# An encoder layer in hi/lo split fp32: the 16x16 substitution of the next head pair becomes a stream of its own, and the state chain of a pair is planned behind it

## The chip, the cores and the metric

The kernel runs on one core of a Trainium2 chip. The metric is device time in microseconds (us), the median of repeated executions. One further execution was profiled, and all rows below come from it.

## The reference, cut to what matters

One layer of a streaming encoder on 576 tokens: 64 that continue a running stream and 512 that open a new one, in nine chunks of 64 tokens. The layer has width 1024, sixteen heads of 64, and everything is in fp32.

```python
h   = rms_norm(x, g_pre_mix)
p   = h @ w_in                    # r, k, v, three low-rank inputs, u, gv, two gates
oA  = rwkv7(p)                    # per head: S = S*w + (S a) b' + v k' ; y = S r
oB  = gmlp(u, gv)                 # spatial gating over 128-frame chunks
m   = sigmoid(gateA) * (oA @ w_proj_a) + sigmoid(gateB) * (oB @ w_proj_b)
x   = x + rms_norm(m @ w_o);  x = x + rms_norm(swiglu(rms_norm(x)))
```

The recurrence of `rwkv7` is computed by chunks. Inside a chunk it needs the inverse of a unit triangular 64x64 matrix per head; between chunks the 64x64 state is carried from one chunk to the next.

## The kernel before, in words

**Products.** Every large product takes three passes on TensorE (PE): each operand is split into a high and a low part, and high x high, low x high and high x low are summed. For the weights, ScalarE (ACT) rounds a raw block to its high part (`whi<-raw`, L302) and GpSimd (POOL) subtracts it in two halves (`wlo<-raw,whi`, L305). One block of 128 columns is 48 matmuls of 288 columns, named `pj` in the first half of the kernel.

**Head pairs.** Heads are worked two at a time, in eight pairs numbered 0 to 7, in roughly the first 520 us; the products `pb`, `gv`, `pa`, `po`, `fg`, `fp` of the rest of the layer follow. For a pair, in order:

- `elementwise`: the decay products `z`, their tanh on ACT (`sg`, `ta`, L666), a running sum along each chunk on VectorE (DVE), `L` (L670), its two exponentials on ACT (`EL` L674, `sg<-L` L676), then `k`, `aq`, `BK`, `AR` and the inner products `am`. DVE masks these into `AB`, and eight DMAs of SyncE (SP) write the diagonal 16x16 blocks of `AB` to DRAM (`d_inv<-AB`, L750).
- `inverse`: SP loads the blocks back, as 80 matrices on 80 partitions (`M`, L855). DVE inverts them by substitution: 15 steps of two small operations, a product `Xt` (L863) and a sum `X` (L866), each dependent on the one before. SP stores `X` to DRAM (L868) and loads it as `IV` in eight DMAs (L872). DVE transposes it (`IT`, L875), and the products `m` (two), `mp`, `mu` build the 64x64 inverse from 16x16 blocks.
- `turns`: transposes on PE (`tb`, `tr`, `tv`) with their copies on ACT (`At`, `Kt`, `Vt`) and DVE (`AB<-tb`, L816), and the products `wv`.
- `batch`: the products `d`, `e`, `c`, `y` of all nine chunks.
- `chain`: the state goes from chunk to chunk. A product `pc` needs the state that DVE's sum before it left (`S`, and `So` for the states that are results, L1005). At the end `py` adds the states' part to the result `Y`.
- `finish`: normalisation and output gate, stored to DRAM.

**What sets the order.** PE's instructions stand in the order in which the class `Weave` writes them. Each of the functions above is a generator, a stream that yields either an estimated time in us, looked up in the table `LAT`, or an event with such a time behind it. `Weave.run` keeps an estimated clock: as long as some stream may go on, it goes on, and otherwise the next matmul of the running weight block is issued as a filler. Nothing of the table exists on the chip; real waits are semaphores. DVE, ACT, POOL and SP get their orders from the framework's scheduler, apart from a few instructions that are pinned, and each runs its queue strictly in that order here.

In the kernel before, `inverse` of pair p+1 holds the substitution too and starts as soon as its `A` event is there (`inv_all`). While the chain of pair p runs, the 30 substitution operations of pair p+1 stand on DVE between the `TD`/`AR` sums of pair p (L966, L967) and the first state sum of the chain (L1005).

Of the kernel before, what the change touches and what calls it, by code (L numbers as in the profile page):

```python
# [20 lines left out]
NPAIR = NH // 2  # L21
# [16 lines left out]
LAT = {  # L38
# [4 lines left out]

# [1 line left out]
}  # L45
# [188 lines left out]
def layer(tc, I, O):  # L234
# [35 lines left out]
    clk = Weave()  # L270
# [110 lines left out]
    d_inv = [tc.dram_tile([2, 2, 64 // SB, 10, SB, SB], F32, name=f"d_inv{g}") for g in range(NPAIR)]  # L381


    EV = [{"hp": p_} for p_ in range(NPAIR)]
# [463 lines left out]
        clk.signal("values", hp_)  # L848


    def inverse(E):

        hp_, AB, di = E["hp"], E["AB"], d_inv[E["hp"]]
        M = rp.tile([P, SB, SB], F32, tag="M", name="M")[0:NU]
        sp.dma_start(M.rearrange("u s t -> u (s t)"), di[0].rearrange("h b u s t -> (h b u) (s t)"))  # L855
        X = rp.tile([P, SB, SB], F32, tag="X", name="X")[0:NU]
        sp.dma_start(X.rearrange("p i t -> p (i t)"), I["cst"][0:NU, C_X0:NCST])
        yield lat("M", hp_)
        tmp = rp.tile([P, SB * SB // 4], F32, tag="Xt", name="Xt")[0:NU]
        for s in range(0, SB - 1):  # L860
            w, r = SB - 1 - s, s + 1
            t3 = tmp[:, 0:r * w].rearrange("u (j t) -> u j t", t=w)
            ins = dve.tensor_tensor(t3, X[:, 0:r, s:s + 1].broadcast_to([NU, r, w]), M[:, s:s + 1, s + 1:SB].broadcast_to([NU, r, w]), ALU.mult)  # L863
            if s == 0:
                tc.keep_in_program_order(ins)
            dve.tensor_tensor(X[:, 0:r, s + 1:SB], X[:, 0:r, s + 1:SB], t3, ALU.add)  # L866
            yield LAT["X"]
        sp.dma_start(di[1].rearrange("h b u s t -> (h b u) (s t)"), X.rearrange("p i t -> p (i t)"))  # L868
        for h in range(2):
            for b in range(64 // SB):  # L870
                r0_ = 64 * h + SB * b
                sp.dma_start(IV[r0_:r0_ + SB, :, SB * b:SB * b + SB], di[1, h, b].rearrange("u s t -> s u t"))  # L872
        blocks = [(64 * h, 64 * h + 32) for h in range(2)]
        quarters = [(64 * h + 32 * b, 32 * b) for h in range(2) for b in range(2)]
        turn = lambda: dve.transpose(IT.rearrange("p c t -> p (c t)"), IV.rearrange("p c t -> p (c t)"))  # L875
        U = AB.rearrange("p j h t -> p (j h) t")
        yield lat("U", hp_)
        if hp_ > 0:
            yield (("d", hp_ - 1), 0.0)

        PT = rp.tile([P, 10, SB], F32, tag="PT16", name="PT16")
        tc.keep_in_program_order(turn())
        yield lat("m1", hp_)
        yield from clk.free()
        pp = ps1("m1", 1.8)[:, 0:10 * SB].rearrange("p (c t) -> p c t", t=SB)
        for u in range(10):
            for r, q in quarters:
                mmul(pp[r:r + 32, u], U[r:r + SB, u, q:q + 32], IT[r:r + SB, u, q:q + SB], start=True, stop=True)
        act.activation(PT, pp, ACT.Copy, scale=low)
        yield lat("m2", hp_)  # L890
        yield from clk.free()
        pp = ps1("m2", 2.2)[:, 0:10 * SB].rearrange("p (c t) -> p c t", t=SB)
        for u in range(10):
            for r, q in quarters:
                mmul(pp[r:r + SB, u], PT[r:r + 32, u, :], IV[r:r + 32, u, q + SB:q + 32], start=True, stop=True)
        for r, q in quarters:
            act.activation(IV[r:r + SB, :, q + SB:q + 32], pp[r:r + SB], ACT.Copy)

        PT = rp.tile([P, 10, 32], F32, tag="PT", name="PT")
        turn()  # L900
        yield lat("mp", hp_)
        yield from clk.free()
        pp = ps1("mp", 1.9)[:, 0:320].rearrange("p (c t) -> p c t", t=32)
        for u in range(10):
            for a0, a1 in blocks:
                mmul(pp[a1:a1 + 32, u], U[a0:a1, u, 32:64], IT[a0:a1, u, 0:32], start=True, stop=True)
        for _, a1 in blocks:
            act.activation(PT[a1:a1 + 32], pp[a1:a1 + 32], ACT.Copy)
        yield lat("mu", hp_)
        yield from clk.free()  # L910
        pp = ps1("mu", 1.9)[:, 0:320].rearrange("p (c t) -> p c t", t=32)
        for u in range(10):
            for _, a1 in blocks:
                mmul(pp[a1:a1 + 32, u], IV[a1:a1 + 32, u, 32:64], PT[a1:a1 + 32, u, :], start=True, stop=True)
        for _, a1 in blocks:
            act.activation(IT[a1:a1 + 32, :, 0:32], pp[a1:a1 + 32], ACT.Copy)
        clk.signal("it", hp_)
# [74 lines left out]
    def chain(E):  # L992


        AR, C, S0, hp_ = (E[n] for n in ("AR", "C", "S0", "hp"))
        add = lambda c: C[:, PLACE[c][1], PLACE[c][0], :]
        state = lambda c: S0 if c == 0 else add(1) if c == 2 else S[:, c, :]
        for n, cs in enumerate([(2, 0)] + [(c,) for c in range(3, NCH)]):
            pc = ps1c("pc").rearrange("p (i v) -> p i v", v=HD)
            for i, c in enumerate(cs):  # L1000
                mmul(pc[:, i], TD[:, c, :], state(c), start=True, stop=True)
            for i, c in enumerate(cs):
                last = c in (0, NCH - 1)
                dst = rp.tile([P, HD], F32, tag="So", bufs=2, name="So") if last else S[:, c + 1, :]
                dve.tensor_tensor(dst, pc[:, i], add(c), ALU.add)  # L1005
                if last:
                    sp.dma_start((O["wkv_s"] if c == 0 else O["wkv_p"])[hp_], dst)
            yield LAT["S"]

        yield (("wide", hp_), LAT["y"])  # L1010
        Y = E["Y"]
        yield from clk.free(2)
        py = [ps1("py", 2.2)[:, 0:320].rearrange("p (j v) -> p j v", v=HD) for _ in range(2)]
        for c, j, half_ in PLACES2:
            for h, rows in enumerate(HR):
                mmul(py[h][HR[half_], j], AR[rows, 1, c * 64:(c + 1) * 64], state(c)[rows], start=True, stop=True, skip_group_check=True)
        for h in range(2):
            dve.tensor_tensor(Y[:, :, HR[h]], py[h], Y[:, :, HR[h]], ALU.add)
        clk.signal("chain", hp_)
# [45 lines left out]
    def elem_all():  # L1065
# [13 lines left out]
        for i in range(2):  # L1079
            sp.dma_start(R["ln"][i][0:64], I["rows"][i:i + 1, :].broadcast_to([64, D]))  # L1080

    def inv_all():
        for p_ in range(NPAIR):
            yield (("A", p_), 0.0)
            yield from inverse(EV[p_])

    def turn_all():
        for p_ in range(NPAIR):
            yield (("A", p_), 0.0)
            yield from turns(EV[p_])  # L1090

    def batch_all():
        for p_ in range(NPAIR):
            yield from batch(EV[p_])

    def chain_all():
        for p_ in range(NPAIR):
            yield (("inv", p_), LAT["ch0"])
            yield from chain(EV[p_])

    def fin_all():
        for p_ in range(NPAIR):
            yield (("chain", p_), 0.0)
            yield from finish(EV[p_])
# [235 lines left out]
    def norm2(h):  # L1340
        hs = HS[h]
        yield (("y", h), 0.0)
        for j in range(8):
            square_sum(mix_q, R["acc2"], y[j][:, hs], j == 0, hs, (dve, pool)[h])
            yield LAT["sq"]
        yield LAT["rs"]
        b = yield from rstd_row(R["fp"], R["acc2"], STARTS[h], "r2")
        act.activation(R["rs2"][:, hs], b, ACT.Copy)
        clk.signal("rs2", h)
# [170 lines left out]
    with tc.manual_schedule(engines={mybir.EngineType.PE}):  # L1520
        lora = {0: lora_w(lora_raw(0), pin=False)}
        for nm, b in (("k", BLK_K), ("r", BLK_R), ("v", BLK_V)):
            take = Shifted(b, nm, scale=True)
            EV[0][nm] = [take(h, raw0[nm][:, HS[h]]) for h in range(2)][1]
            clk.signal(nm, 0)
        clk.run(chain_all(), fin_all(), batch_all(), inv_all(), turn_all(), elem_all(), norm1(0), norm1(1), norm2(0), norm2(1), hidden(), oa_all(), ob_all(),
                ln_all(), norm3(0), norm3(1))
    R["o"].close()
    R["d0"].close()
# [19 lines left out]
```

## Time and profile before

| | us |
|---|---|
| median of 3 runs | 1224.84 |
| lowest and highest run | 1223.98, 1225.69 |
| profiled execution, its own time | 1224.46 |
| its span, first to last instruction | 1222.7 |
| PE busy | 1179.5 |
| POOL busy | 606.8 |
| DVE busy | 524.5 |
| ACT busy | 467.9 |

The own time is what the same execution would report as a run; the span leaves out 1.76 us around the instructions. A busy time is the sum over an engine's instructions, and PE's idle time is mostly made of short waits, which a view of the trace lists by the instruction that ended them.

### The profile page before, as it was taken

What the parts mean: (1) busy time and instruction counts of PE and PEld (TensorE: products, weight loads), DVE (VectorE), ACT (ScalarE), POOL (GpSimd) and SP (SyncE); (2) the same over time, 40 slices, a digit from 0 to 9 for tenths busy, and PEclk for the clock granted to TensorE, in tenths of its full rate; (3) what the DMA queues carried; (4) which work ended last, traced back from release to release, by engine and by line L of the source; (5) the groups of instructions that cost most, each with busy time, mean ns of one, the idle gap of its engine ahead of it and who ended that gap; (6) DMA issues with size and microseconds to landing.
All of it is one profiled execution on the core that took longest, in us unless ns stands there. A gap on an engine that the chain in (4) does not pass through costs nothing.

```text
span 1222.7 us, 29954 instructions
## 1 busy us (share of the span) xinstructions
PE 1179.5 (96%) x12938; PEld 1146.6 (94%) x12938; DVE 524.5 (43%) x1086; ACT 467.9 (38%) x889; POOL 606.8 (50%) x477
## 2 busy tenths in 40 slices
PE   7999999999999999999899999999999999999997
PEld 6999889899998999999899999999999999999996
DVE  5756365656555655432515431753333333300003
ACT  5555534453545453342521333543222222222220
POOL 6675343546363535233545553466555655634442
PEclk9999999999999999999999999999999999999999
DMA  5234223232322223242643541232222222242222
GB/s 186 75 111 106 78 55 94 48 94 50 97 68 76 75 77 87 89 132 77 210 125 122 182 147 55 94 111 81 87 87 79 78 87 86 81 157 83 80 77 78
DMA packets 68276, 118.05 MB, mean 97 GB/s; under 512 B 30832, under 2 KB 36208, under 8 KB 68144
## 3 DMA queue, kind: packets, MB, share of 16 engines
q1 hardware_dynamic: 68000, 116.06, 31.7%
q8 instruction: 101, 1.65, 0.6%
q14 instruction: 31, 0.25, 0.1%
q10 hardware_dynamic: 144, 0.08, 0.0%
HBM read 99.83 MB, written 16.28 MB: 95 GB/s over the span
## 4 chain that ended last, share of the span: by engine, by line
PE 78%; DVE 12%; ACT 4%; issue 3%; POOL 2%; DMA 1%; SPq 0%; DVEq 0%; POOLq 0%; ACTq 0%
PE fg L286 21%; PE pj L286 15%; PE po L286 15%; PE pb L286 4%; PE gv L286 4%; PE pa L286 3%; PE fp L286 2%; DVE X L866 2%; DVE Xt L863 2%; PE am L286 1%; PE z L286 1%; PE m L286 1%; PE pc L286 1%; PE wv L286 1%; PE d L286 1%
## 5 line engine op out<-in xcount | busy, mean ns | idle before, releaser
L305 POOL TENSOR_TENSOR wlo<-raw,whi 128x512 fp32r<-128x512 f32 (+1 forms) x286 | 395.4, 1407 | 344.2 <-ACT whi L302 322.3
L302 ACT ACTIVATE whi<-raw 128x1024 fp32r<-128x1024 f32 x143 | 149.0, 1045 | 282.0 <-PE fg L286 174.9
L1293 DVE TENSOR_TENSOR rs<-rs,nsq 128x288 f32<-128x288 f32 (+2 forms) x12 | 9.0, 752 | 105.9 <-ACT nsq L1292 105.9
L1365 DVE TENSOR_TENSOR ft<-ft,fg 128x288 f32<-128x288 f32 x40 | 16.4, 450 | 68.0 <-PE fg L286 66.5
L1359 DVE TENSOR_TENSOR fg<-fg,rs 128x288 f32<-128x288 f32 x40 | 16.5, 453 | 63.0 <-PE fg L286 62.9
L1362 DVE SCALAR_TENSOR_TENSOR ft<-ft,fg 128x576 f32<-128x576 f32 (+1 forms) x24 | 28.1, 1172 | 18.3 <-ACT ft L1361 18.3
L1363 POOL TENSOR_TENSOR ft<-ft,rs 128x576 f32<-128x576 f32 (+1 forms) x24 | 31.8, 1327 | 6.5 <-DVE ft L1362 5.8
L368 POOL TENSOR_TENSOR rr<-rm,mhalf 128x3 f32<-128x3 f32 (+1 forms) x6 | 5.0, 831 | 51.9 <-DVE rm L367 51.9
L286 PE MATMUL pc<-S,TD 128*128 128x64 f32 x112 | 20.2, 262 | 8.6 <-DVE So L1005 8.6
L688 POOL TENSOR_TENSOR aq<-aq,k 128x576 f32<-128x576 f32 x8 | 11.4, 1425 | 34.4 <-PE pc L286 30.0
L286 PE MATMUL pj<-h1h,whi 128*128 128x288 f32 x88 | 27.8, 316 | 0.0
L286 PE MATMUL pj<-h5h,whi 128*128 128x288 f32 x88 | 27.8, 316 | 0.0
L286 PE MATMUL pj<-h0h,whi 128*128 128x288 f32 x88 | 27.7, 315 | 0.0
L863 DVE TENSOR_TENSOR Xt<-X,M 80x15 f32<-80x15 f32 (+7 forms) x120 | 25.5, 213 | 5.1 <-DMA M<-d_inv 1.5
L286 PE MATMUL pj<-h2h,whi 128*128 128x288 f32 x88 | 27.7, 315 | 0.0
L286 PE MATMUL pj<-h6h,whi 128*128 128x288 f32 x88 | 27.5, 312 | 0.0
L286 PE MATMUL pj<-h7h,whi 128*128 128x288 f32 x88 | 27.3, 311 | 0.0
L286 PE MATMUL pj<-h4h,whi 128*128 128x288 f32 x88 | 27.2, 309 | 0.0
L286 PEld LDWEIGHTS pc<-S,TD 128*128 128x128 f32 x112 | 17.4, 189 | 10.3 <-DVE So L1005 10.3
L866 DVE TENSOR_TENSOR X<-X,Xt 80x15 f32<-80x15 f32 (+7 forms) x120 | 25.3, 210 | 4.1
L1036 POOL TENSOR_TENSOR gm<-gm,mhalf 128x10 f32<-128x10 f32 x8 | 16.1, 2012 | 21.9 <-DVE gm L1035 12.7
L286 PE MATMUL pj<-h3h,whi 128*128 128x288 f32 x88 | 26.8, 305 | 0.0
(1200 smaller groups left out, 4269.6 us busy)
## 6 DMA issues: line engine op xcount, KB each, us to landing
raw<-in_w_in SPq DMA_DIRECT2D x50, 512.0 KB, 3.7
raw<-in_w_gate SPq DMA_DIRECT2D x22, 512.0 KB, 3.6
raw<-in_w_up SPq DMA_DIRECT2D x22, 512.0 KB, 3.6
raw<-in_w_down SPq DMA_DIRECT2D x16, 512.0 KB, 3.5
raw<-in_w_gv SPq DMA_DIRECT2D x8, 512.0 KB, 4.2
raw<-in_w_proj_a SPq DMA_DIRECT2D x8, 512.0 KB, 4.1
raw<-in_w_proj_b SPq DMA_DIRECT2D x8, 512.0 KB, 3.7
raw<-in_w_o SPq DMA_DIRECT2D x8, 512.0 KB, 3.7
```

Source lines behind the costliest of these rows:

```text
L286: return pe.matmul(out, lhsT, rhs, **kw)
L302: keep(act.activation(hi[:, :cols], raw[:, :cols], ACT.Copy))
L305: keep(pool.tensor_tensor(lo[:, c0:c1], raw[:, c0:c1], f(hi[:, c0:c1]), ALU.subtract))
L688: pool.tensor_tensor(aq, aq, k, ALU.mult)
L863: ins = dve.tensor_tensor(t3, X[:, 0:r, s:s + 1].broadcast_to([NU, r, w]), M[:, s:s + 1, s + 1:SB].broadcast_to([NU, r, w]), ALU.mult)
L866: dve.tensor_tensor(X[:, 0:r, s + 1:SB], X[:, 0:r, s + 1:SB], t3, ALU.add)
L1036: pool.tensor_tensor(m, m, mhalf, ALU.pow)
L1293: eng.tensor_tensor(acc[:, hs], acc[:, hs], q[:, hs], ALU.add)
L1359: keep(dve.tensor_tensor(g[:, HS[h]], pg, rs2[:, HS[h]], ALU.mult))
L1362: keep(dve.scalar_tensor_tensor(t[:, ts], t[:, ts], 1.0, g[:, ts], ALU.add, ALU.mult))
L1363: pool.tensor_tensor(t[:, ts], t[:, ts], rs2[:, ts], ALU.mult)
L1365: dve.tensor_tensor(t[:, HS[h]], t[:, HS[h]], pu, ALU.mult)
```

## The change

The substitution leaves `inverse` and becomes `substitute`, a stream of its own, which ends in the event `x` of its pair. `inverse` of a pair starts at that event. `chain` of pair p waits in the plan for `x` of pair p+1 as well. In the table the wait for `M` becomes 11.0 us (9.0), a substitution step 0.65 (0.75), the wait from the `IV` loads to the first transpose 2.5 + 12.0 (11.0), and the chain's first wait 6.5 (6.0). No instruction is added or removed on PE; the order changes, and with it the places of the fillers.

```diff
-    "M": 9.0, "X": 0.75, "U": 11.0, "m1": 2.3, "m2": 2.4, "mp": 4.2, "mu": 2.0, "d0": 2.2, "e0": 3.1, "y0": 3.5,
-    "ch0": 6.0, "S": 1.8, "y": 0.5, "gn1": 4.0, "gn2": 6.0, "to": 3.5, "to1": 0.45, "g": 1.8,
+    "M": 11.0, "X": 0.65, "O": 2.5, "U": 12.0, "xc": 0.0, "m1": 2.3, "m2": 2.4, "mp": 4.2, "mu": 2.0, "d0": 2.2, "e0": 3.1, "y0": 3.5,
+    "ch0": 6.5, "S": 1.8, "y": 0.5, "gn1": 4.0, "gn2": 6.0, "to": 3.5, "to1": 0.45, "g": 1.8,
...
-    def inverse(E):
-
-        hp_, AB, di = E["hp"], E["AB"], d_inv[E["hp"]]
+    def substitute(E):
+
+        hp_, di = E["hp"], d_inv[E["hp"]]
...
         sp.dma_start(di[1].rearrange("h b u s t -> (h b u) (s t)"), X.rearrange("p i t -> p (i t)"))
+        clk.signal("x", hp_)
+
+    def inverse(E):
+
+        hp_, AB, di = E["hp"], E["AB"], d_inv[E["hp"]]
+        yield LAT["O"]
         for h in range(2):
...
+    def sub_all():
+        for p_ in range(NPAIR):
+            yield (("A", p_), 0.0)
+            yield from substitute(EV[p_])
+
     def inv_all():
         for p_ in range(NPAIR):
-            yield (("A", p_), 0.0)
+            yield (("x", p_), 0.0)
             yield from inverse(EV[p_])
...
             yield (("inv", p_), LAT["ch0"])
+            if p_ + 1 < NPAIR:
+                yield (("x", p_ + 1), LAT["xc"])
             yield from chain(EV[p_])
```

DVE's queue where the chain of pair 2 begins, before (the first two rows are the last step of pair 3's substitution, L1005 are the chain's sums):

```order
L863 TENSOR_TENSOR Xt<-X,M 80x15
L866 TENSOR_TENSOR X<-X,Xt 80x15
L1005 TENSOR_TENSOR S<-pc,C 128x64
L1005 TENSOR_TENSOR So<-pc,C 128x64
L1005 TENSOR_TENSOR S<-pc,C 128x64
L489 SCALAR_TENSOR_TENSOR k<-pj,omm,q 128x288
L1005 TENSOR_TENSOR S<-pc,C 128x64 x2
L489 SCALAR_TENSOR_TENSOR r<-pj,omm,q 128x288
```

The same place in the changed kernel, where the chain's sums are line 1011:

```order
L863 TENSOR_TENSOR Xt<-X,M 80x15
L866 TENSOR_TENSOR X<-X,Xt 80x15
L489 SCALAR_TENSOR_TENSOR k<-pj,omm,q 128x288
L670 SCALAR_TENSOR_TENSOR L<-rmask,sg 128x576
L489 SCALAR_TENSOR_TENSOR k<-pj,omm,q 128x288
L1011 TENSOR_TENSOR S<-pc,C 128x64
L1011 TENSOR_TENSOR So<-pc,C 128x64
L816 TENSOR_TENSOR AB<-tb,rn 128x8x64
L816 TENSOR_TENSOR AB<-tr,rn 128x2x64
L1011 TENSOR_TENSOR S<-pc,C 128x64
L720 TENSOR_TENSOR BK<-aq,sg 128x576
```

The running sum `L`, both halves of the next pair's `k`, the two `AB<-tb` products and `BK` have come between the substitution and the chain's sums or into the chain.

ACT's queue at the same place before (`C` are the chunk products' results):

```order
L302 ACTIVATE whi<-raw 128x1024
L666 ACTIVATE sg<-z,half 128x288
L668 ACTIVATE sg<-sg,chalf 128x576
L674 ACTIVATE EL<-L 128x9x64
L676 ACTIVATE sg<-L 128x576
L970 ACTIVATE C<-c 128x256
L970 ACTIVATE C<-c 128x320
```

And at the copies of `C` in the changed kernel, where they are line 976 (`Y<-y` are results of the products `y`):

```order
L976 ACTIVATE C<-c 128x256
L976 ACTIVATE C<-c 128x320
L430 ACTIVATE st<-pj 128x288
L302 ACTIVATE whi<-raw 128x1024
L993 ACTIVATE Y<-y 128x256 x2
```

The rounding of a weight block has moved from ahead of the copies of `C` to behind them. `EL`, which needs `L`, now stands thirteen rows further down, behind the first turned `At`:

```order
L818 ACTIVATE At<-tb 128x512
L674 ACTIVATE EL<-L 128x9x64
L819 ACTIVATE At<-tr 128x128
L676 ACTIVATE sg<-L 128x576
L666 ACTIVATE ta<-z,half 128x288
L484 ACTIVATE shc<-pj 128x1
L485 ACTIVATE q<-pj,vec 128x288
L302 ACTIVATE whi<-raw 128x1024
L818 ACTIVATE Kt<-tb 128x512
L819 ACTIVATE Kt<-tr 128x128
L686 ACTIVATE aq<-ta,nkk 128x576
```

What stands behind `EL` there, a second weight block, the turned `Kt` and `aq`, now waits for `L`, and so for the substitution. On PE the first `pc` of a chain comes later behind `c` (counts are in the prediction), `tb` stands ahead of it, and the first `m` of the next pair's inverse comes right behind `py`.

## Rows read from the trace of the kernel before

**Rows 1.** The page's busy times of the engines.

```profile
PE 1179.5 (96%) x12938; PEld 1146.6 (94%) x12938; DVE 524.5 (43%) x1086; ACT 467.9 (38%) x889; POOL 606.8 (50%) x477
```

**Rows 2.** PE's waits: releaser; total us, times, longest.

```profile
PE pc L286 <- DVE So L1005: 8.6, 7, 1.8
...
PE m L286 <- DVE IT L875: 1.8, 3, 1.0
...
PE m L286 <- ACT whi L302: 1.5, 1, 1.5
PE gv L286 <- POOL wlo L305: 1.4, 2, 1.1
PE gv L286 <- ACT whi L302: 1.4, 1, 1.4
...
PE pa L286 <- ACT s L448: 1.3, 1, 1.3
PE z L286 <- ACT AB L936: 1.2, 1, 1.2
```

**Rows 3.** Timeline of PE: chain of pair 0, of pair 2, of pair 6.

```profile
157.98 0.43 PE L286 MATMUL pc<-S,TD 128*128 128x64 f32 x2 [0.29 <-DVE So L1005]
...
264.66 0.39 PE L286 MATMUL c<-AB,At 64*64 64x128 f32 x4
...
271.76 0.33 PE L286 MATMUL pc<-C,TD 128*128 128x64 f32 x2
...
276.12 0.43 PE L286 MATMUL pc<-S,TD 128*128 128x64 f32 x2 [1.77 <-DVE So L1005]
276.39 0.60 PE L290 MATMUL tb<-cst,AR 128*128 128x128 f32 x4
...
286.11 1.43 PE L286 MATMUL wv<-Vt,AK 64*64 64x64 f32 x40
...
508.34 0.43 PE L286 MATMUL pc<-S,TD 128*128 128x64 f32 x2 [1.73 <-DVE So L1005]
```

**Rows 4.** Timeline of DVE at the same place: start us, us.

```profile
264.19 1.36 DVE L670 TENSOR_TENSOR_SCAN L<-rmask,sg 128x576 f32<-128x576 f32 x1 [4.38 <-ACT sg L668]
...
268.45 0.16 DVE L863 TENSOR_TENSOR Xt<-X,M 80x15 f32<-80x15 f32 x1
...
275.63 0.18 DVE L866 TENSOR_TENSOR X<-X,Xt 80x15 f32<-80x15 f32 x1
...
275.85 0.21 DVE L1005 TENSOR_TENSOR So<-pc,C 128x64 f32<-128x64 f32 x1
...
276.73 0.51 DVE L489 SCALAR_TENSOR_TENSOR k<-pj,omm,q 128x288 f32<-128x288 f32 x1
...
282.73 1.49 DVE L720 TENSOR_TENSOR BK<-aq,sg 128x576 f32<-128x576 f32 x1
```

**Rows 5.** Windows over tile X, substitutions of pairs 3 and 7: DVE busy, count.

```profile
268.40:275.90 7.50, 6.04 (x30) 1.00 0.15 60
...
499.00:508.10 9.10, 8.00 (x30) 1.00 0.10 34
```

**Rows 6.** Timelines of ACT and POOL beside pair 7's substitution.

```profile
500.68 1.05 ACT L302 ACTIVATE whi<-raw 128x1024 fp32r<-128x1024 f32 x1
...
501.81 2.60 POOL L305 TENSOR_TENSOR wlo<-raw,whi 128x512 fp32r<-128x512 f32 x2 [8.69 <-ACT whi L302]
```

**Rows 7.** Timelines of ACT and POOL, chain of pair 2.

```profile
265.64 0.69 ACT L674 ACTIVATE EL<-L 128x576 f32<-128x576 f32 x1 [1.49 <-DVE L L670]
...
268.97 0.49 ACT L666 ACTIVATE ta<-z,half 128x288 f32<-128x288 f32 x1
...
278.31 1.41 POOL L688 TENSOR_TENSOR aq<-aq,k 128x576 f32<-128x576 f32 x1
```

**Rows 8.** Windows: all engines' busy time and counts, PE clock; fillers and a half-clock stretch.

```profile
179.60:183.00 3.40, 3.40 (x68) 3.09 (x60) 1.66 (x4) 1.02 (x2) 1.25 (x1) 0.50 0.02 5
...
690.00:720.00 30.00, 30.00 (x228) 30.00 (x226) 12.98 (x20) 9.93 (x11) 18.26 (x14) 1.00 0.55 173
```

More of the change, by code (lines that the diff above doesn't have):

```diff
@@ L1525, in layer @@
             clk.signal(nm, 0)
-        clk.run(chain_all(), fin_all(), batch_all(), inv_all(), turn_all(), elem_all(), norm1(0), norm1(1), norm2(0), norm2(1), hidden(), oa_all(), ob_all(),
+        clk.run(chain_all(), fin_all(), batch_all(), inv_all(), sub_all(), turn_all(), elem_all(), norm1(0), norm1(1), norm2(0), norm2(1), hidden(), oa_all(), ob_all(),
                 ln_all(), norm3(0), norm3(1))
```

## The prediction

> **What bounds the kernel now.** The page's busy times come first: PE is busy for 1179.5 of 1222.7 us, the other engines for half of that or less [rows 1]. So nothing is won by making another engine faster in general; what can be won is PE's idle time, 43 us, and next PE's time at half clock. The view of PE's waits, grouped by releaser, says which idle time this change can reach [rows 2]. The largest group there that belongs to the head pairs is `pc` behind DVE's sum `So`: 8.6 us in seven waits, one for each pair but the last. The waits of `m` behind `IT` (1.8) and behind a weight rounding (1.5), of `z` behind the copies of `AB` (1.2), and, behind the pairs, of `gv` (1.4 and 1.4) and `pa` (1.3) are smaller. Waits at the start of the layer and in the feed-forward part are not touched.
>
> Next the timelines of PE and DVE at one chain, that of pair 2 [rows 3, 4]. I call C the end of its last `c`, 264.66 + 0.39 = 265.05. The first `pc` runs at 271.76, C+6.7. The second wants to start at 276.12 - 1.77 = 274.35, C+9.3, and starts at C+11.1. In that time DVE runs the 30 operations of pair 3's substitution, from 268.45 to 275.81, and then `S` and `So`; `So` ends at 276.06 and `pc` follows 0.06 later. So the chain waits for an inversion that it doesn't need. Of the 7.36 us of the substitution 6.04 are its own operations [rows 5], one `k` of 0.5 [rows 4] stands between, and the rest are the gaps between dependent operations. Pair 6 waits 1.73 for the same reason, pair 0 only 0.29 [rows 3], so pairs 1 to 5 hold 8.6 - 1.73 - 0.29 = 6.6 us.
>
> A filler costs 30.00 / 228 = 0.132 us [rows 8]. The number of matmuls is the same before and after, so moving fillers costs nothing by itself; only waits and clock change the sum.
>
> **The change, part by part.** Counts are from the instruction orders, durations from the rows.
>
> *The chain's start in pairs 1 to 5.* Before, 30 fillers, 4 `z` and the products `y` stand between `c` and the first `pc`; 34 x 0.132 = 4.5 and the measured 6.7 leave 2.2 for `y`. After, it is 66 fillers, 4 `bo`, 8 `z` (78 x 0.132 = 10.3), `y` (2.2) and two of the groups `tb`, at 0.60 [rows 3] each: 13.7. Behind the two first `pc` (0.4) come a third `tb` (0.6) and 12 fillers (1.6), so that the next `pc` wants to start at C+16.3, seven later than before.
>
> DVE's side: the scan `L` (1.36) no longer stands ahead of the `TD`/`AR` sums, so the substitution starts at 268.45 - 1.36, C+2.0. It takes 7.36 - 0.5 = 6.9, and two bonus products inside it, taken at 0.5 as `k`: C+9.9 if nothing else slows it. But in the changed order ACT's weight rounding comes right behind the copies of `C`, so that POOL's two `wlo` fall beside the substitution. Before, that happened in pair 7's substitution alone: rounding at 500.68, `wlo` from 501.81 for 2.60 [rows 6], and there the same 30 operations took 8.00 instead of 6.04 [rows 5]. I take those 1.96: C+11.8. Then, in DVE's new order, `k` (0.5) and `L` (1.36), C+13.7. ACT follows with `EL` (0.69), the rest of `At` (0.2, estimate), `sg` (0.69), `ta` (0.49), and the two operations of the second `k` (0.5) [rows 7], 2.6 together: C+16.3. DVE's second `k` (0.5), `S` and `So` (0.4) end at C+17.2. The second `pc` waits 0.9, against 1.3 before; without POOL beside the substitution it would have 1.1 to spare.
>
> Two later waits are possible in the same chain, because everything on ACT behind `EL` is late as well. Behind the rounding (1.05), two copies of `Kt`, `aq`, a square, `ta`, one `q` and two copies of `Vt`, some 5.4 by the durations above less 0.1 of overlap at each of nine, `Vt` ends near C+20.8; `wv` wants it at C+17.2 + 0.3 + 0.7 + 1.6 + 0.3 + 0.8 = C+20.9 (two `pc`, `tv`, 18 fillers). That is nothing to 0.8; I take 0.3. And POOL runs `wlo` (2.60, from C+17.4) ahead of `aq` (1.41 [rows 7]), then DVE `BK` (1.49) and half of `r` (0.5) ahead of the next sum (0.2): C+23.6. The fourth `pc` wants to start behind `wv` (1.43 [rows 3]) and ten small products, C+23.3: wait 0.3. Together 1.5 for each pair. The bounds are 0 (no slowing by POOL) and 2.6 (all three at their upper ends). Five pairs: 7.5 instead of 6.6, a **loss of 0.9**.
>
> *Pair 6.* The pair behind it is the last, so after the substitution DVE and ACT have no `L`, `EL`, `k` to do; 79 fillers and `bo`, `y` and three `tb` put the first `pc` at C+14.4, and the substitution ends by C+11.8. **Gain 1.7**, the whole wait. Pair 0 is left at its 0.3.
>
> *The inverse.* The first `m` now stands right behind `py`, and `IT` ahead of the sums of `Y`. The last `pc` is followed by 15 fillers (2.0) and `py`, and `IT` needs the last sum and its own transposition, under 1.5 together, so the wait behind `IT` should go. The waits behind a rounding and of `z` hang on the place of single instructions, which all move. Of 1.8 + 1.5 + 1.2 = 4.5 I take a **gain of 3.5** (2 to 4.5). Covers that get thinner: `mp` waits for a second `IT`, which now stands behind the reduction of ACT's square, and `to` for the normalised `Y`. I count both as level to within half a us, 0.2 for each of six pairs: a **loss of 1.2** (0 to 4).
>
> *The end of the pairs.* The last `py` comes 12 fillers earlier within the `gv` stretch, 1.6 us, and the normalisation, store and reload of pair 7 with it. `gv` and `pa` wait 1.4 + 1.4 + 1.3 = 4.1 for ACT and POOL, which that work holds up. I take half, a **gain of 2.0** (0 to 4.1).
>
> *Clock.* From 179.6 on PE ran 3.40 us at a granted clock of 0.50 [rows 8], right behind the 1.5 us wait of `m`. At the full clock that stretch would be 1.7 shorter. With that wait gone it may stay away, and another wait may bring one: **gain 0.8** (0 to 1.7).
>
> Sum: -0.9 + 1.7 + 3.5 - 1.2 + 2.0 + 0.8 = 5.9. Against the profiled execution's 1224.46 (its span is 1222.7; the median of the runs, 1224.84, lies 0.4 higher) that gives **1218.6**.
>
> One rule of the Trainium skill speaks against the change, and it is not in the sum. The page "SBUF — State Buffer", section "SBUF: two separate sides", says that VectorE and GpSimd take a shared pair of ports as an exclusive lock, for an operation with two SBUF inputs against a GpSimd operation that reads SBUF, and that the loser blocks for the whole instruction. By that, the substitution would lose all of POOL's 2.60 and not 1.96, 0.64 more in each of five pairs, and the time would be 1218.6 + 3.2 = 1221.8. Pair 7's rows bear the rule out in kind and show three quarters of its size.
>
> **The rivals.** *POOL stays clear of the substitution:* if the weight block arrives late or is taken earlier, `wlo` runs beside something else, as in pairs 1 to 6 now. Then DVE and ACT are 2 us earlier throughout, all three waits go, and the time is 1218.6 - 7.5 = 1211.1. For it speaks that the substitution of pair 3 ran without POOL; against it, that ACT's new order has the rounding exactly where pair 7 had it. Chance 0.18.
>
> *No effect:* the chain was only planned later, and the resources it needs were moved later with it. With 2.3 of waits in each of the five pairs (5 x 0.8 more) and the gain at the inverse gone to waits of the same kind elsewhere (3.5 less, with the 1.2 of new ones not counted twice), the time is 1218.6 + 4.0 + 3.5 - 1.2 = 1224.9. For it speaks that each wait before is short, so that a little lateness restores it. Chance 0.22.
>
> *Slower, through ACT:* the second weight rounding stands on ACT behind `EL` and ahead of `Kt`, `aq` and `Vt`. If its raw block isn't there when ACT comes to it, ACT stands, and `wv`, `BK` and the sums behind them are late by as much, in each of five pairs. To be slower by over 0.2% takes 1227.3 - 1218.6 = 8.7, so 1.7 for each pair decides. A delay as long as one block's subtraction, 2.60 [rows 6], which would free the buffer for that block, gives 1218.6 + 5 x 2.6 = 1231.6. Against it: SP's order issues that load before the substitution's store. Chance 0.15.
>
> **How the numbers follow.** My forecast has 0.45, with a range of its own from 1215 to 1222. A measurement of this kernel tells a change from none at about 0.2%, 2.4 us: faster is below 1222.4, slower above 1227.3. Faster: 0.40 of the forecast, 0.18 of the first rival, 0.04 of the second, 0.62. The same: 0.05 and 0.18, 0.23. Slower: 0.15. The range goes from the first rival's 1211.0 to the upper edge of no effect, 1227.5, and leaves the slower case out.
>
> **What would show it.** In the profile after, substitutions of pairs 2 to 6 with POOL's `wlo` beside them and 8 us busy instead of 6 confirm the contention; 6 us and no `pc` wait, the first rival. The first state sum at C+17 confirms the path through `L`, `EL` and `k`; at C+14 I have put work on it that runs beside it. Waits of `wv` behind `Vt`, or of `pc` behind a sum that follows `BK`, show the later ones. The wait of `m` behind `IT` should be gone from the view of waits, that of pair 6's `pc` too, and those of `gv` and `pa` be about half. What would make the prediction wrong is a new wait that recurs in every pair and isn't in this list, above all on ACT at a rounding, or half-clock stretches behind new waits.

## The result, and the profile after

| | before | after |
|---|---|---|
| median of 18 runs (us) | 1224.82 | 1231.16 |
| lowest and highest | 1217.85, 1226.52 | 1224.27, 1233.43 |
| first `pa` product in the trace (us) | 609.16 | 615.11 |

The changed kernel is slower: the ratio of the times is 1.005, with a 95% interval from 1.0033 to 1.0067. The first `pa` comes right behind the head pairs and their `gv` products, so its start measures the part of the layer that the change touches: 5.95 us later. Its rows, before and after:

```profile
609.16 0.54 PE L286 MATMUL pa<-m0h,whi 128*128 128x288 f32 x2 [1.31 <-ACT s L448]
```

```profile
615.11 0.53 PE L286 MATMUL pa<-m0h,whi 128*128 128x288 f32 x2 [0.47 <-ACT s L448]
```

The page's engine line of the changed kernel, against [rows 1]:

```profile
PE 1185.0 (96%) x12938; PEld 1152.1 (94%) x12938; DVE 548.7 (45%) x1086; ACT 466.8 (38%) x889; POOL 603.3 (49%) x477
```

DVE is busy 24 us longer with the same 1086 instructions, of which 13 us lie in the eight substitutions (63.6 us after, 50.8 before, by windows over tile `X`), and PE 5.5 us longer with the same matmuls. PE's waits in the changed kernel (releaser, total us, times, longest), against [rows 2]:

```profile
PE y L286 <- DVE bonus L790: 11.9, 6, 2.3
...
PE am L286 <- ACT IV L903: 4.8, 6, 1.1
PE tr L290 <- ACT At L819: 1.6, 1, 1.6
...
PE gv L286 <- POOL wlo L305: 1.2, 2, 0.9
...
PE pa L286 <- ACT s L448: 0.5, 1, 0.5
PE mp L286 <- DVE AB L743: 0.5, 1, 0.5
```

The waits that the change was to remove are gone, all of them: `pc` behind `So` (8.6 before), `m` behind `IT` and the rounding, `z` behind the copies. In their place stand two that recur in nearly every pair, `y` behind a bonus product of DVE and `am` behind ACT's copies into `IV`; `tr` and `mp` wait once each.

The place of the first, in the chain of pair 2: timelines of DVE, POOL and PE.

```profile
262.22 0.16 DVE L863 TENSOR_TENSOR Xt<-X,M 80x15 f32<-80x15 f32 x1
...
264.25 1.26 DVE L866 TENSOR_TENSOR X<-X,Xt 80x55 f32<-80x55 f32 x1
265.54 1.19 DVE L863 TENSOR_TENSOR Xt<-X,M 80x60 f32<-80x60 f32 x1
266.76 0.22 DVE L866 TENSOR_TENSOR X<-X,Xt 80x60 f32<-80x60 f32 x1
266.90 0.45 DVE L790 TENSOR_TENSOR bonus<-bo,v 128x288 f32<-128x288 f32 x1
```

```profile
264.17 2.49 POOL L305 TENSOR_TENSOR wlo<-raw,whi 128x512 fp32r<-128x512 f32 x2 [6.46 <-ACT whi L302]
```

```profile
264.39 0.73 PE L286 MATMUL y<-Vt,AK 64*64 64x64 f32 x24
267.40 0.55 PE L286 MATMUL y<-Vt,AK 64*64 64x64 f32 x10 [2.28 <-DVE bonus L790]
```

POOL's two subtractions begin at 264.17. The two substitution operations beside them take 1.26 and 1.19 us, where their neighbours take 0.2. Behind them on DVE stands the bonus product, which reads `bo` out of PSUM; it ends at 267.35, and 0.05 later `y`, which has already begun in other banks, goes on. Nothing that `y` reads comes from the bonus. The program hands out four PSUM banks in turn. Each of the two `bo` products holds one of them until its bonus product has read it, and `y` takes three, so its last bank is one of theirs. From this I took it that `y` waited for the bank; e1 tries it.

What PE's clock does around that wait (windows: us, busy time and count of PE, of its weight loads, of DVE, ACT, POOL, then the granted clock):

```profile
265.20:267.40 2.20, 0.00 (x0) 0.00 (x0) 2.13 (x5) 0.00 (x0) 1.46 (x2) 1.00 0.00 0
267.90:271.30 3.40, 3.40 (x55) 3.28 (x48) 2.99 (x15) 1.61 (x6) 0.00 (x0) 0.50 0.39 153
272.00:275.00 3.00, 3.00 (x25) 3.00 (x25) 1.78 (x2) 2.20 (x4) 0.26 (x1) 1.00 0.14 31
```

PE is idle for 2.2 us, then works for 3.4 us at the lower of its two levels, 1.2 GHz, and then at full clock again. Fillers in the slow stretch start 0.24 us apart, 0.13 behind it. Four of the five long waits of `y` are followed by such a stretch; before, there were two stretches between the start of the pairs and `pa`, at 179.6 [rows 8] and 592.6. The length of a wait alone doesn't decide it: of the waits before, that of `m` at 179 (1.5 us) was followed by a slow stretch, and that of `pc` at 276 (1.77 [rows 3]) was not.

### The profile page after: what moved, and what is told of

The parts are those of the page before. It is cut to its first block, busy times and chain, and to the rows that moved or that the text cites. A ratio compares the mean times of both kernels' runs of the same rounds, so it can differ in the third digit from the quotient of the medians.

```text
span 1229.2 us, 29962 instructions
## 1 busy us (share of the span) xinstructions
PE 1185.0 (96%) x12938; PEld 1152.1 (94%) x12938; DVE 548.7 (45%) x1086; ACT 466.8 (38%) x889; POOL 603.3 (49%) x477
## 4 chain that ended last, share of the span: by engine, by line
PE 81%; DVE 11%; ACT 4%; issue 2%; DMA 1%; POOL 1%; POOLq 0%; ACTq 0%; DVEq 0%; SPq 0%
PE fg L286 21%; PE pj L286 17%; PE po L286 15%; PE gv L286 4%; PE pb L286 4%; PE pa L286 3%; PE fp L286 2%; PE z L286 2%; DVE X L866 1%; DVE Xt L863 1%; PE am L286 1%; PE pc L286 1%; DVE TD L972 1%; PE wv L286 1%; PE d L286 1%
## 5 line engine op out<-in xcount | busy, mean ns | idle before, releaser
L866 DVE TENSOR_TENSOR X<-X,Xt 80x15 f32<-80x15 f32 (+7 forms) x120 | 32.3, 269 | 3.9
L863 DVE TENSOR_TENSOR Xt<-X,M 80x15 f32<-80x15 f32 (+7 forms) x120 | 31.3, 261 | 4.9 <-DMA M<-d_inv 1.3
L822 POOL TENSOR_TENSOR AR<-eye,eC 128x576 f32<-128x576 f32 x8 | 9.4, 1177 | 47.3 <-PE tr L290 47.3
L702 POOL TENSOR_TENSOR rmul<-cst,rn 128x1280 f32<-128x1280 f32 x8 | 19.0, 2379 | 22.8 <-DVE S L1011 21.0
L1011 DVE TENSOR_TENSOR S<-pc,C 128x64 f32<-128x64 f32 x48 | 10.2, 212 | 44.3 <-PE pc L286 44.3
L286 PE MATMUL am<-AR,BK 64*64 64x128 f32 x640 | 23.9, 276 | 4.8 <-ACT IV L903 4.8
```

The lines of the kernel that those rows point to most:

```text
L286: return pe.matmul(out, lhsT, rhs, **kw)
L702: pool.tensor_tensor(rmul.rearrange("p j h t -> p (j h) t"), mask.unsqueeze(1).broadcast_to([P, 10, P]), rn.unsqueeze(2).broadcast_to([P, ...
```

## The experiments

Each kernel was run beside the kernel before on the same chip, and the ratio is against that. "First `pa`" is 609.16 before and 615.11 after.

| run | median us | ratio to before, interval | first `pa` us |
|---|---|---|---|
| e1, `bo` copied by ACT | 1228.74 | 1.006, 1.0037 to 1.0083 | 612.59 |
| e2, after, no subtraction | 1209.15 | 0.9909, 0.9881 to 0.9937 | 593.29 |
| e3, before, no subtraction | 1217.40 | 0.9975, 0.9948 to 1.0001 | 602.91 |
| e4, no chain wait | 1243.71 | 1.0182, 1.0141 to 1.0224 | 627.49 |
| e5, after, X in PSUM | 1212.39 | 0.992, 0.989 to 0.995 | 596.51 |
| e6, before, X in PSUM | 1224.72 | 1.0022, 0.9994 to 1.005 | 611.18 |
| e7, table only | 1259.76 | 1.0297, 1.0262 to 1.0332 | 640.94 |
| e8, longer hold of `bo` | 1236.19 | 1.0119, 1.0084 to 1.0154 | 620.08 |

The theory: POOL's subtraction, which the new order puts beside the substitution, stops DVE; the bonus inside the substitution is late; it holds a PSUM bank, and PE waits for that. The rivals: `y` waits for something else; the bonus is late because of its place, POOL or no POOL; the longer set times do the harm.

**e1: take the bank away from the bonus.** ACT copies `bo` out of PSUM, DVE multiplies the copy.

```diff
-            dve.tensor_tensor(bonus[:, hs], sb[:, 0:HALF], v[:, hs], ALU.mult)
+            act.activation(bonus[:, hs], sb[:, 0:HALF], ACT.Copy)
+            dve.tensor_tensor(bonus[:, hs], bonus[:, hs], v[:, hs], ALU.mult)
```

> The changed kernel with one edit: the sum products bo are copied out of PSUM by ScalarE, and VectorE multiplies the copy in place; PE's order and VectorE's order stay as they are. Theory A (the waits of y, 11.9 us in six, come from a PSUM bank that bo holds until VectorE reaches the bonus product inside the substitution, which GpSimd's subtraction has stopped): the waits of y fall from 11.9 to under 2 us, the half-clock stretches right behind them go, some waits of pc come back (0.5 to 1 us in each of five pairs, since VectorE is late all the same), and the time is 1218 to 1222. Theory B (y waits for something else that ends at the same moment, as the copies of C or Vt): the waits of y stay near 12 us and the time at 1231.

The waits of `y` are gone from the list, so it was the bank. The time is not: 1.006 is no better than the changed kernel's 1.005, and the expected 1218 to 1222 was missed. The first `pa` comes only 2.5 us sooner. Three half-clock stretches, which I had expected to go, are there, each behind a wait of `tr`. Its waits, and the place of the new one in the timelines of PE, ACT and DVE:

```profile
PE tr L290 <- ACT At L820: 15.3, 5, 3.2
...
PE am L286 <- ACT IV L904: 4.9, 6, 1.1
```

```profile
275.43 0.33 PE L290 MATMUL tr<-cst,BK 128*128 128x128 f32 x1 [2.99 <-ACT At L820]
...
274.53 0.69 ACT L674 ACTIVATE EL<-L 128x576 f32<-128x576 f32 x1 [3.45 <-DVE L L670]
275.12 0.26 ACT L820 ACTIVATE At<-tr 128x128 f32<-128x128 f32 x1
...
272.57 0.18 DVE L867 TENSOR_TENSOR X<-X,Xt 80x15 f32<-80x15 f32 x1
272.67 0.51 DVE L489 SCALAR_TENSOR_TENSOR k<-pj,omm,q 128x288 f32<-128x288 f32 x1
273.09 1.34 DVE L670 TENSOR_TENSOR_SCAN L<-rmask,sg 128x576 f32<-128x576 f32 x1
```

ACT stands for 3.45 us at `EL`, which needs `L`, which stands on DVE behind the substitution; the copy `At<-tr` is behind `EL`, and the next transposes go to the PSUM tile that it reads. With the first bank free, the late substitution stops PE at the next one. So the bank of `bo` was where the lateness came out, not where it came from. The edit is not quite clean, though. PE comes sooner here, so another operation of POOL, `AR` (L822, 1.21 us from 270.63), starts beside the substitution, one more of its operations takes 1.03 us, and the 30 take 8.92 instead of 8.07:

```profile
262.00:273.00 11.00, 8.92 (x30) 1.00 0.22 77
```

So some 0.9 of the 2.99 us that `tr` waits are of this run's own making (an estimate from the two sums).

**e2 and e3: take POOL's subtraction away, from both kernels.** The filler blocks of the pairs use their high part in place of the low one.

```diff
-        return item(need, [I["w_in"][blk]], body)
+        return (need, lambda: [wraw(I["w_in"][blk])], lambda raws, pin=True: [wone(r, pin) for r in raws], body)
+    def wone(rawc, pin):
+        raw, cols = rawc
+        hi = wp.tile([P, KD * P], F32R, tag="whi", bufs=WB, name="whi")
...
+        return hi, hi
```

> The changed kernel without GpSimd's subtraction for the weight blocks that serve as fillers in the head pairs: the high part stands in for the low part in the third pass, so the projections of those blocks lack the low parts of their weights, and the number of instructions on PE stays. Theory A (contention of GpSimd and VectorE makes the bonus late): the 30 substitution operations take 6.1 us instead of 8.07 in pairs 3 to 7, the waits of y go to under 0.5 us each, no pc waits either, and the time is 1211 to 1216. Theory B (the bonus is late because twelve substitution operations stand ahead of it, with GpSimd or without): the waits of y fall by less than half, the time stays above 1224.

> The kernel before with the same work left out: no subtraction for the low parts of the filler blocks of the head pairs, the high part stands in. It gives the change's worth without GpSimd beside it. Theory A: GpSimd was hardly beside the substitution here, so the waits of pc stay at 7 to 9 us and the time is 1220 to 1224, some 8 us above the changed kernel with the same edit. Theory B: both kernels gain alike, and the changed one stays slower by 4 to 6 us.

Windows over the substitution (DVE's busy time in its 30 operations), first of the changed kernel, then of e2:

```profile
262.00:272.00 10.00, 8.07 (x30) 0.83 0.22 84
```

```profile
260.50:268.60 8.10, 6.05 (x30) 1.00 0.31 103
```

In e2 the substitution takes 6.05 us, the waits of `y` are 1.0 us in four, `pc` and `am` don't appear, `tr` waits 0.3 once, and no half-clock stretch lies between 80 us and the end of the feed-forward part. In e3 the waits of `pc` stay (6.6 us in five). Both times lie below the expected ranges (1209.15 for 1211 to 1216, 1217.40 for 1220 to 1224), and `pc` below its 7 to 9; the difference between the two is the one expected. The same change that costs 6 us with the subtraction gains 8.2 us without it (1217.40 - 1209.15), and the first `pa` comes 9.6 us sooner. The place of the bonus alone doesn't do the harm. This pair of runs leaves work out and so shortens other things too; e5 doesn't.

**e5 and e6: all the work, but out of POOL's way.** X lies in the spare columns of the PSUM bank of `pc`; each operation reads one operand from SBUF and one from PSUM.

```diff
-        X = rp.tile([P, SB, SB], F32, tag="X", name="X")[0:NU]
-        sp.dma_start(X.rearrange("p i t -> p (i t)"), I["cst"][0:NU, C_X0:NCST])
+        X = R["px"][0:NU, P:P + SB * SB].rearrange("u (i t) -> u i t", t=SB)
+        act.activation(X, R["x0"], ACT.Copy)
...
+        Xs = rp.tile([P, SB, SB], F32, tag="X", name="Xs")[0:NU]
+        dve.tensor_copy(Xs, X)
...
-            pc = ps1c("pc").rearrange("p (i v) -> p i v", v=HD)
+            pc = R["px"][:, 0:P].rearrange("p (i v) -> p i v", v=HD)
```

> The changed kernel with the matrix X of the substitution held in the unused columns of the PSUM bank of pc instead of SBUF, so that each of the 30 operations reads one operand from SBUF and one from PSUM; ScalarE sets the identity there ahead of time and VectorE copies X out at the end (about 0.3 us). All work of the reference is done, and the orders of PE, GpSimd and VectorE stay. Theory A (VectorE is stopped by GpSimd only where both operands lie in SBUF): the sum of the 30 operations falls from 8.07 to 6 to 7 us with the subtraction still beside them, the waits of y behind the bonus fall from 11.9 to under 2 us, no waits of tr behind At take their place, and the time is 8 to 14 us below the changed kernel's, so 4 to 8 us (0.3 to 0.7%) below the kernel before. Theory A': only the sums escape and the products don't, or both stay blocked: 7.5 to 8.1 us, waits of y over 6 us, no gain on the kernel before.

> The kernel before with X in PSUM in the same way. Here GpSimd is beside the substitution of pair 7 alone, so if X in PSUM is no slower by itself the waits of pc stay at 7 to 9 us and the time is within 3 us of the kernel before; if the operations on PSUM are slower (7 us and more for the 30), the waits of pc grow by that in each pair and it is 3 to 8 us slower.

In e5, the windows of the 15 products and of the 15 sums, POOL's row beside them, and the waits:

```profile
257.50:265.50 8.00, 3.00 (x15) 1.00 0.31 104
...
257.50:265.50 8.00, 3.13 (x15) 1.00 0.31 104
```

```profile
259.82 2.51 POOL L305 TENSOR_TENSOR wlo<-raw,whi 128x512 fp32r<-128x512 f32 x2 [6.46 <-ACT whi L302]
```

```profile
PE am L286 <- ACT IV L909: 4.9, 6, 1.1
...
PE tr L290 <- ACT Kt L819: 2.2, 4, 0.8
...
PE y L286 <- DVE bonus L790: 1.1, 4, 0.3
```

The subtraction runs beside the substitution as in the changed kernel and takes as long (2.51 us), and the 30 operations take 6.13 us together, as if it weren't there. The bonus products stand where they stood, behind the same twelve operations. The waits of `y` fall from 11.9 to 1.1 us, no half-clock stretch lies between 20 and 770 us, and the kernel is 0.8% faster than the one before (0.5 to 1.1%): 10.5 us, where I had expected 4 to 8. So the change did take away the waits it was meant for, and the contention took the gain back. That settles the cause. In e6 the time, 1.0022, is not told apart from no change. It has no gain from X in PSUM, but it isn't a pure test of that either: the substitution and the chain's products share a bank there, the 30 operations still take 6.06 us but are spread over 14.7 us, with the chain's sums between them, and PE waits about as long as it waited for `So` before:

```profile
PE px L286 <- DVE px L870: 6.8, 8, 1.8
...
PE px L286 <- DVE Xs L873: 1.3, 2, 1.0
```

**e4: the stream without the chain's wait.**

```diff
-            if p_ + 1 < NPAIR:
-                yield (("x", p_ + 1), LAT["xc"])
             yield from chain(EV[p_])
```

> The changed kernel without the chain's wait for the next pair's substitution in the plan; the substitution stays a stream of its own and the table keeps its new times. PE's order goes back towards that of before: bo ahead of c, the first pc 8 us earlier. Theory A (the harm comes from the bonus products that this wait moved from ahead of c to behind it): no waits of y behind the bonus, the waits of pc behind the sums come back with 1 to 2 us each, and the time is 1222 to 1228. Theory B (the harm comes from the longer set times of the table): the time stays at 1229 to 1233.

Both expectations missed: 1243.71. No wait of `y` behind the bonus, as theory A had it, but also hardly any of `pc`; the substitution came to lie between other work of DVE, and PE waits in other places, of which these are the largest:

```profile
PE m L286 <- DVE IT L881: 4.9, 5, 1.9
PE pa L286 <- ACT s L448: 4.8, 1, 4.8
PE m L286 <- ACT gq L1038: 4.5, 2, 4.1
PE d L286 <- DVE X L866: 4.2, 1, 4.2
```

How much of this is the substitution's doing, no run shows. So this run doesn't tell what the chain's wait is worth: one wait less in the plan gives another order altogether.

**e7: the table alone,** on the kernel before.

```diff
-    "M": 9.0, "X": 0.75, "U": 11.0, "m1": 2.3,
+    "M": 11.0, "X": 0.65, "U": 14.5, "m1": 2.3,
-    "ch0": 6.0, "S": 1.8,
+    "ch0": 6.5, "S": 1.8,
```

> The kernel before with the new times of the table alone (M 11.0, X 0.65, U 14.5 for the two new waits together, ch0 6.5), without the new stream and without the chain's wait. The substitution stays ahead of the chain's first sum on VectorE. Theory: the waits of pc behind the sums stay at 6 us or more, the rest moves at random, and the time is 1218 to 1232 where the kernel before has 1219 to 1225. If it falls below the kernel before by over 4 us, the table and not the stream held the gain that was expected.

```profile
PE pc L286 <- DVE So L1005: 22.2, 5, 7.8
```

As expected, the chain's sums stay behind the substitution, but at a far higher price than I gave (1259.76, expected 1218 to 1232): more of DVE's other work fell between its operations and more of POOL's beside them, and in pairs 4 to 6 the 30 take 12.2 to 12.4 us where the kernel before has 6.1. The numbers of the table are no gain without the stream.

**e8: the planner told of the long hold.**

```diff
-            sb = ps1("bo", 2.0)
+            sb = ps1("bo", 6.0)
```

> The changed kernel with one number of the plan changed: the bank of a bo product is taken to be held for 6.0 us instead of 2.0, near what the trace shows (262.18 to 267.40). The planner then moves bo and the products around it. Theory A: no waits of y behind the bonus; since the subtraction still stops the substitution, ScalarE's late EL and At show elsewhere, with waits of tr, wv or pc of 5 to 10 us in all, and the time is 1220 to 1230. If it comes out below 1216, the planner's number was the whole fault.

The waits of `y` behind the bonus are gone, as expected; `tr`, `wv` and `pc` wait 5.4 us together, within the 5 to 10 expected. But the largest wait is now of `d` behind DVE's output gate (9.6 us in three), and the time, 1236.19, lies above the expected range. One number changed and the whole order went another way, so the run says that the number alone is no remedy, and not more.

**e9 and e10: two more traces of the changed kernel.**

> The changed kernel once more, for a second trace of it. Its 18 runs lie in two groups, 1224 to 1227 and 1229 to 1233. Theory A (the groups differ in how many of the five waits of y, some 2.3 us each, are followed by 3.4 us of PE at half clock, 1.7 us lost each): a trace near 1231 shows four such stretches in the head pairs, one near 1225 none or one, with the waits of y at 11 to 12 us in both. Theory B: in the lower group the waits of y are shorter.

> The same kernel again, with the same expectation as the run before: four half-clock stretches in the head pairs at about 1231, none or one at about 1225, waits of y 11 to 12 us in both.

Both runs took 1230.3 us, with four half-clock stretches in the pairs and waits of `y` of 11.9 us each, as theory A had it for that time. The lower group was not caught, so theory A against B stays open. But the two differ inside. In e10 three of the half-clock stretches in the pairs have twice the length, 6.8 us, and the first `pa` comes at 618.97 against 614.28. The stretch from there to the last product of the norm is the same program; windows of e10, then of e9:

```profile
619.00:1219.60 600.60, 596.30 (x4490) 592.03 (x4490) 189.73 (x316) 176.59 (x256) 308.76 (x232) 0.99 0.32 100
```

```profile
614.30:1219.60 605.30, 601.00 (x4490) 596.70 (x4490) 190.25 (x316) 176.50 (x256) 309.19 (x232) 1.00 0.31 99
```

The same 4490 matmuls take 596.3 or 601.0 us. The difference lies in stretches that are full in both, here a window of the feed-forward part, again of e10 and then of e9:

```profile
900.00:930.00 30.00, 30.00 (x233) 30.00 (x233) 10.40 (x15) 8.60 (x10) 18.01 (x12) 1.00 0.26 81
```

```profile
900.00:930.00 30.00, 30.00 (x228) 30.00 (x227) 10.10 (x15) 8.69 (x10) 16.46 (x12) 1.00 0.28 89
```

At a granted clock of 1.00 in both, e10 runs 233 matmuls where e9 runs 228, and 2591 against 2548 from 850 to 1190 us; 43 more are some 5.7 us (estimate, 43 x 0.133). Why the pace differs, no run shows. So two executions with the same time can differ by 4.7 us in the pairs and make it up behind them, where the change has no part. Whether the two groups of runs come from this stretch, I can't say; that it alone can move a time by as much as the change is shown.

## Why the prediction was wrong, step by step

I forecast 1218.6, a gain of 5.9; it lost 6.3. The range, from 1211.0 to 1227.5, left the result out.

- *The substitution with POOL beside it* was right: it starts at C+1.7 (forecast C+2.0; C is 260.56 here) and ends at 271.80, C+11.2 (forecast C+11.8), and takes 8.07 us where I had 8.00 from pair 7 [rows 5].
- *The step that failed* is the next one, "two bonus products inside it, taken at 0.5 as `k`". I counted them as DVE's time and asked only what that does to the chain's sums behind them. I didn't ask who waits for them. They free the banks of `bo`, and in the new order `y` follows `bo` by a few fillers; so the 2 us came out in front of `y`, 2.0 to 2.3 us in each of pairs 2 to 6 and 0.8 in pair 1, 11.9 together. My sum has no term for this wait; it stood at nothing. My sum had the price of the contention as 1.5 for each pair at `pc`, `wv` and the later sums. There it was nothing: PE came to the first `pc` at 278.10, C+17.5 instead of C+13.7, after the wait and the slow stretch, and DVE and ACT were ready.
- *The sign that I had named for the path,* the first state sum at C+17, seemed to come true: it is at C+18.1. That was luck. The sum waited 0.76 for PE's `pc` and not for DVE's own work:

```profile
278.68 0.23 DVE L1011 TENSOR_TENSOR S<-pc,C 128x64 f32<-128x64 f32 x1 [0.76 <-PE pc L286]
```

- *The path through `L`, `EL` and the ACT queue* exists, as e1 shows, but it comes out at `tr`, again at a place in PSUM that has to come free, and with about 3 us a pair, of which some 0.9 is e1's own. I had looked at the data that `wv` reads and not at the banks that ACT's copies free.
- *New waits* were priced at 1.2 with bounds 0 to 4. `am` behind `IV` alone is 4.8, and with `tr` (1.6) and `mp` (0.5) it is 6.9, so this term was too small by 5.7. For `am` the timelines of PE and ACT show the same kind of thing:

```profile
243.12 0.44 PE L286 MATMUL am<-AR,BK 64*64 64x128 f32 x6 [0.81 <-ACT IV L903]
...
241.23 0.74 ACT L1038 ACTIVATE gq<-Y 128x640 f32<-128x640 f32 x1 [1.82 <-DVE Y L1036]
241.87 1.20 ACT L903 ACTIVATE IV<-m 16x160 f32<-16x160 f32 x4
```

  `am` reads neither `gq` nor `IV`; the copies of `m` into `IV` end at 243.07, behind the square of the pair before, and 0.05 later `am` goes on. That it is the bank of `m` was argued from this, not tried.
- *The clock* was entered as a gain of 0.8 and is a loss. The busy and idle time of PE from 60 us to the first `pa` shows it, windows of the kernel before and of the changed one:

```profile
60.00:609.10 549.10, 528.29 (x8115) 501.23 (x8113) 291.99 (x724) 258.22 (x575) 256.98 (x207) 0.99 0.31 90
```

```profile
60.00:615.00 555.00, 533.14 (x8113) 506.20 (x8111) 314.59 (x720) 255.81 (x574) 253.17 (x206) 0.99 0.31 89
```

  Idle time went from 20.8 to 21.9 us, busy time from 528.3 to 533.1. The waits that went and the waits that came cancel nearly; most of the 5.95 us is the same matmuls taking 4.9 us longer. Two stretches of 3.4 us more, in which a filler takes 0.24 instead of 0.13, account for about 3 of these (2 x 3.4 x 0.45); the rest I can't place.
- *What held:* the waits of `pc` in pair 6, of `m` and of `z` are gone (5.2 forecast for `pc` of pair 6, `m` and `z` together, 6.2 found), and `gv` and `pa` fell from 4.1 to 1.7 where I had half of it.
- *The first rival,* POOL clear of the substitution, is what e2 built on purpose; in e5 POOL stays beside the substitution but no longer slows it. The rival gave 1211.1 against 1224.46 before, 1.1% less. e2 has 0.9%, of which 0.25%, not clear of the noise, is there in e3 too, without the change, and e5 has 0.8%, with `am` and `tr` still waiting.
- *The slower rival* named ACT standing at its second rounding. ACT isn't seen waiting there: the rounding follows `q` at 277.24 without a gap. Its side was right, its mechanism wrong, and that its 1231.6 lies next to the measured 1231.16 is luck.
- *Small things in the working:* the bound of 2.6 for each pair names three upper ends but states only two, and the ends of the range, 1211.0 and 1227.5, stand as 1211.1 and 1227.3 where they come from. Neither bears on the outcome.

The Trainium skill's page "SBUF — State Buffer" says, in the section "SBUF: two separate sides", that a VectorE operation with two SBUF inputs and a GpSimd operation that reads SBUF exclude each other: the one that starts first holds the shared ports for its whole instruction. The rows agree: two subtractions of 1.25 us, two substitution operations stretched to 1.26 and 1.19. From it I had worked out a loss of all of POOL's time, 2.60; measured is 2.0 of 2.5. The two operations that are stopped would have taken 0.2 each anyway, and 2.49 - 2 x 0.2 = 2.1 is near that (an estimate from these rows). The same page, in the section "Who interferes with whom", says that a VectorE instruction with at most one SBUF input, outside the modes that use both ports, doesn't contend with GpSimd. The trace of e5 agrees, with 6.13 us beside the subtraction.

## What to carry to other kernels

When an instruction is moved into a long dependent run on another engine, list what its completion frees, PSUM banks first, and find who takes that next in the new order; the data it produces are only half of its readers. When two streams of one schedule meet, read from the new queues which GpSimd work falls beside which VectorE work, and if both read SBUF, try one operand of the dependent run in PSUM before giving up the order; here that took the ratio from 1.005 to 0.992. And a wait of two microseconds in a full PE stream can cost more than itself: four of five here had 3.4 us at half clock behind them.

## What the runs showed of the hardware that I had not expected

One VectorE operation of 0.2 us with both operands in SBUF takes 1.2 us beside a GpSimd subtraction, but at 80 partitions with one operand in PSUM it keeps its 0.2 us; PSUM is not slower here (6.13 against 6.05 us for the 30). The same 4490 matmuls behind the pairs took 596.3 us in one execution of a kernel and 601.0 in another, at a granted clock of 0.99 and 1.00, and in a window with 1.00 in both, 233 against 228 ran in 30 us. And the stretch at half clock behind the same wait of 2.28 us was 3.4 us long in one execution and 6.8 in another.
